# Two-layer streaming encoder on one core: mixer keys set anew, cache rows written from loaded tiles

## The chip, the cores and the metric

One core of a Trainium2 chip runs the whole program; the metric is the device time of one launch in microseconds. The five instruction queues are TensorE (PE), VectorE (DVE), ScalarE (ACT), GpSimd (POOL) and SyncE (SP). In this kernel SP issues every transfer.

## The reference

Two layers act on a prompt of 1024 frames and on a sample batch of 8 streams with 16 frames each. Everything is float32 with 1024 model columns. Cut to what matters:

```python
def trunk_layer(x, ...):
    xn = rms_norm(x, norm_mix)
    q, k, v, u = mixer_inputs(xn, pos, w_in, q_gain, k_gain)
    keys = jnp.concatenate([cache_k, k], axis=1)      # sample; the prompt has no cache
    vals = jnp.concatenate([cache_v, v], axis=1)
    attn = sink_attention(q, keys, vals, sinks, None) # prompt: a window of chunks
    pool, new_pool = pool_mixer(u, pool_prev, w_pool, pool_scale)
    x = x + jnp.concatenate([attn, pool], axis=-1) @ w_out
    f, new_conv = conv_ffn(rms_norm(x, norm_ffn), conv_prev, w_up, conv_w, conv_b, w_down)
    return x + f, keys[:, -WINDOW:], vals[:, -WINDOW:], new_pool, new_conv
```

The last line names what the change touches: for the sample, the new cache of each layer is the newest 112 of the 128 old rows, followed by 16 new ones. The old rows are read for the attention anyway.

## The kernel before, in words

The 1152 rows (1024 prompt, 128 sample) are nine tiles of 128. Each float32 product is made of three TensorE products of rounded high and low parts (`mm3`, L154 to L156), so each weight is split on its way in: a raw block (tag raw, 5 buffers of 256 KB) is cast on ACT (L184) or DVE (L182) to its high part, and DVE takes the low part (L185). The pair (tag W, 6 buffers of 512 KB) is written to DRAM scratch (L188, `wd0k` and the like) and read back from there for the next blocks of tiles (L179).

A layer runs as a **mixer**, then **up**, then **down**. The mixer takes the tiles in three blocks of three: norm (n1 to n3; x tiles loaded at L247, scaled at L258, transposed at L278), key/value/query projections (k0 to k2), pooling input and pooling (u0 to u2, p0 to p2; L448), attention (steps L, per tile: scores L592/L593, masked maximum on DVE L596, exponential on ACT L608, division on DVE L621, transposes L631, value product L644), output projection (o0 to o2) and the second norm (m0 to m2). For the sample tile the scores are at L712, the division at L727, its transposes at L735, the value product at L752; its caches are loaded at L668 and L672. Up and down are products after Strassen's scheme: up forms sums of x halves (s0 and s1; casts L314, subtractions L315, sums L323), multiplies, and adds up the seven products on DVE (L927); down's raw blocks are loaded at L1068 (`wt_load`) and L1078 and split by L1106/L1107, and the hidden rows are split by ACT L1133 and DVE L1134. Layer 0's last ten down units run at the start of layer 1's mixer.

**What sets the order.** The program of a mixer is a list of tokens, each with a key from `PLAN`: `k0=(a, b)` means that step i of stream k0 has the key a + b·i. `arrange` sorts by key as far as prerequisites and buffer limits allow. Then a scheduler sets the order of each engine's queue from that program, and it may hoist an instruction far ahead: the cache copies of both layers stand at 22 to 30 us of the run. PE, DVE and ACT work through their queues in order. SP too: a transfer whose wait is not over holds everything behind it. A transfer also waits for the one eight places ahead of it, since there are eight completion semaphores, used in turn. PSUM has four mm buffers, two s and two tr.

In each `PLAN` entry `e_w` gives how many of every four weight casts go to DVE; `e_k`, `e_u` and their like choose between DVE and ACT for the copies of one step.

Of the kernel before, what the change touches and what calls it, by code (L numbers as in the profile page):

```python
# [44 lines left out]
def arrange(tokens, limits):  # L45
# [17 lines left out]


PLAN = [
    dict(k0=(-17.62, 0.24), u0=(10.61, 1.71), k1=(30.79, 2.26), u1=(78.0, 4.62), o0=(92.76, 2.89), k2=(148.67, 0.53), u2=(167.09, 2.77), o1=(177.0, 4.18), o2=(235.82, 4.28), p0=(40.1, 4.11), p1=(87.53, 9.52), p2=(194.05, 11.9), n1=(-17.77, 3.16), n2=(24.42, 3.62), n3=(92.75, 0.67), m0=(218.99, 3.57), m1=(259.62, 0.1), m2=(181.18, 1.22), d=(4.13, 4.36), L=(26.9, 49.72, 64.52, 85.1, 108.8, 144.29, 159.45, 183.94, 209.44, 245.41), cw=(276.93, 6.24), sc=(242.61, 32.45), s0=(252.65, 2.67), s1=(279.21, 6.7), v=(236.08, 0.18), w=(265.61, 1.32), upw=(297.57, 0.58), e_q=0, e_k=1, e_v=1, e_u=0, e_k2=0, e_qt=0, e_pt0=0, e_pt1=1, e_ps0=1, e_ps1=1, e_ks=0, e_w=1, e_x0=0, e_x1=0, e_x2=1),
    dict(k0=(-52.3, 0.11), u0=(39.12, 0.62), k1=(27.74, 4.1), u1=(77.36, 4.61), o0=(81.16, 2.69), k2=(144.54, 0.53), u2=(154.52, 4.44), o1=(176.58, 5.19), o2=(244.07, 2.25), p0=(50.25, 5.11), p1=(72.82, 0.77), p2=(195.1, 13.29), n1=(-13.38, 2.12), n2=(30.2, 4.39), n3=(93.86, 2.01), m0=(219.6, 1.94), m1=(237.49, 1.8), m2=(278.02, 1.14), d=(-26.81, 5.35), L=(26.9, 49.72, 64.52, 87.91, 107.72, 142.58, 160.43, 180.13, 216.19, 239.71), cw=(266.26, 12.19), sc=(271.63, 4.65), s0=(264.1, 2.05), s1=(266.18, 3.7), v=(283.58, 0.14), w=(284.07, 11.47), upw=(287.29, 0.87), e_q=1, e_k=1, e_v=0, e_u=1, e_k2=0, e_qt=0, e_pt0=0, e_pt1=0, e_ps0=1, e_ps1=1, e_ks=0, e_w=1, e_x0=0, e_x1=1, e_x2=0),
]


# [1 line left out]
def encoder_kernel(ctx: ExitStack, tc: tile.TileContext, consts, x_prompt, x_sample, cache_k, cache_v,  # L72
# [4 lines left out]
    pe, act, dve, pool, sync = nc.tensor, nc.scalar, nc.vector, nc.gpsimd, nc.sync  # L77
# [583 lines left out]
    def sample(l):  # L661
        H = {}
        t = 8
        pr = prep(l, 8)

        def load():
            H["ck"] = T("B", [128, 8, 128])
            sync.dma_start(out=H["ck"], in_=cache_k[l].rearrange("b t g d -> t b (g d)"))  # L668

        def loadv():  # L670
            H["cv"] = T("B", [128, 8, 128])
            sync.dma_start(out=H["cv"], in_=cache_v[l].rearrange("b t g d -> t b (g d)"))  # L672
# [525 lines left out]
    def down_units(l):  # L1198
        us = []
        for u, (j, p) in enumerate(DSEQ):  # L1200
            n = 5 if j in (0, 1, 5, 6) else 4
            late = j == 5 and l < DEPTH - 1
            loads, splits = ((0, 2, 4, 5, 6), (0, 0, 2, 4, 5)) if n == 5 else ((0, 2, 4, 6), (0, 0, 2, 4))

            def f(u=u, j=j, p=p, n=n, late=late, loads=loads, splits=splits):
                if u == 0:
                    down_x(l, 0)
                if u + 2 < len(DSEQ):
                    g_load(l, u + 2)
                if u + 1 < len(DSEQ):  # L1210
                    down_x(l, u + 1)
                    g_split(l, u + 1)
                down_add(l, u, None)
                if j < 6 and not late:
                    for x in range(*(splits + (6,))[p:p + 2]):
                        wd_split(l, j + 1, x)
                    for x in range(*(loads + (6,))[p:p + 2]):
                        wd_load(l, j + 1, x)
                if j == 0:
                    for x in range(p, 6 if p == 4 else p + 1):  # L1220
                        wt_load(l, x)
# [23 lines left out]
    def params1(l):  # L1245
        def f():
            if "own" not in state:
                state["own"] = True
                dve.tensor_reduce(out=own, in_=ident.rearrange("p (b t) -> p b t", t=16), axis=mybir.AxisListType.X, op=ALU.add)
            sync.dma_start(out=gain[:, 0], in_=q_norm[l].partition_broadcast(128))  # L1250
            sync.dma_start(out=gain[:, 1], in_=k_norm[l].partition_broadcast(128))
            sync.dma_start(out=snk[:, 0], in_=attn_sinks[l].partition_broadcast(128))
            for h in range(8):
                sync.dma_start(out=snk[h * 16:(h + 1) * 16, 2, 0:1], in_=attn_sinks[l, h:h + 1].partition_broadcast(16))
            r = T("D", [4, 128])
            sync.dma_start(out=r, in_=pool_scale[l].rearrange("(g p) -> g p", p=128))
            dve.tensor_scalar(out=gain[:, 0], in0=gain[:, 0], scalar1=HD ** -0.5, scalar2=None, op0=ALU.mult)
            dve.tensor_scalar(out=snk[:, 1], in0=snk[:, 0], scalar1=-1.0, scalar2=None, op0=ALU.mult)
            dve.tensor_scalar(out=snk[:, 3, 0:1], in0=snk[:, 2, 0:1], scalar1=-1.0, scalar2=None, op0=ALU.mult)
            tr = P("tr")  # L1260
            pe.transpose(out=tr[:, 0:4], in_=r, identity=ident[0:4, 0:4])
            act.copy(out=pscol, in_=tr[:, 0:4])
        return f
# [71 lines left out]
        x_load(0, [1, 2])()  # L1335
        sync.dma_start(out=cst[:, C_M:C_END], in_=consts[:, C_M:C_END])

    def copies(l):
        def f():
            sync.dma_start(out=nk_s[l, :, 0:112], in_=cache_k[l, :, 16:128])  # L1340
            sync.dma_start(out=nv_s[l, :, 0:112], in_=cache_v[l, :, 16:128])
        return f

    events = []
    pend = []
    for l in range(DEPTH):
        pl = PLAN[l]
        toks = []

        def add(name, key, unit, pre=(), res=None):  # L1350
            toks.append(Token(key, name, unit if isinstance(unit, Unit) else Unit(unit), tuple(pre), res))
# [155 lines left out]
```

## Time and profile before

| | before |
|---|---|
| median of 3 runs | 2243.28 us (2240.95 to 2246.43) |
| the profiled execution | 2242.44 us, span 2240.7 us |
| mean granted clock of TensorE over the span | 0.988 |
| PE busy | 2169.5 us, 97% |
| DVE, ACT, POOL busy | 1712.6 (76%), 943.5 (42%), 326.6 (15%) |
| bytes moved | 389.64 MB, 174 GB/s mean |

Along the span: layer 0's mixer takes 0 to about 420 us, up to 880, down to about 1120; layer 1's mixer (with the end of layer 0's down) to about 1510, up to 1980, down to the end. A row of the timeline gives start, length, engine, line, operation, output <- input, and in brackets how long the engine had been idle and what released it. A granted clock of 1.00 is the full 2.4 GHz, and 0.91 is a mean of stretches at 2.4 and at 1.2 GHz.

### The profile page before, as it was taken

The page shows a single profiled execution, that of the slowest core. Times are in us where ns is not written, and L with a number is a line of the kernel's source. Part 1 is how long each engine was busy: PE and PEld are TensorE (multiplying, and loading weights), DVE is VectorE, ACT ScalarE, POOL GpSimd, SP SyncE. Part 2 cuts the span into 40 slices and gives each one's busy share as a digit, 9 for nine tenths or more (in the row PEclk, how much of TensorE's full clock was granted, in tenths as well). Part 3 has the DMA queues.
Part 4 walks back from the last instruction along what each step waited for, and adds up shares of the span by engine and source line. Part 5 has one row for each costly group of instructions (what it writes and reads, how often), then busy time and mean ns, then how long its engine had stood idle before and what let it go on. Part 6 is the DMA issues. An engine that isn't in the chain of part 4 may idle for free.

```text
span 2240.7 us, 36002 instructions
## 1 busy us (share of the span) xinstructions
PE 2169.5 (97%) x13178; PEld 1945.5 (87%) x13178; DVE 1712.6 (76%) x3234; ACT 943.5 (42%) x1749; POOL 326.6 (15%) x499
## 2 busy tenths in 40 slices
PE   7999999899999999999999999979999999999999
PEld 6867777899999999878888887779999999988887
DVE  4776467989899998867557754689989999987663
ACT  3454345534343434443335543554343434353341
POOL 0000001121213232000000000111212233320000
PEclk9999999899999999999999999999999999999999
DMA  8757565122224346958765665532222343488663
GB/s 313 255 194 269 182 218 173 59 95 79 95 88 151 117 151 220 298 178 268 243 228 184 230 230 207 205 116 84 94 82 93 110 140 128 143 274 267 182 199 113
DMA packets 315940, 389.64 MB, mean 174 GB/s; under 512 B 21906, under 2 KB 219746, under 8 KB 315730
## 3 DMA queue, kind: packets, MB, share of 16 engines
q1 hardware_dynamic: 315762, 387.33, 52.2%
q8 instruction: 104, 1.70, 0.3%
q14 instruction: 74, 0.61, 0.1%
HBM read 279.71 MB, written 109.37 MB: 174 GB/s over the span
## 4 chain that ended last, share of the span: by engine, by line
PE 85%; DMA 6%; DVE 5%; ACT 2%; issue 1%; SPq 0%; POOL 0%; DVEq 0%; ACTq 0%
PE mm L154 15%; PE mm L155 15%; PE mm L156 15%; PE s L156 11%; PE s L154 11%; PE s L155 11%; PE s L644 2%; DMA raw<-in_w_down_dram 1%; DMA raw<-in_w_in_dram 1%; PE tr L631 1%; PE mm L448 1%; DMA W<-wd1o 1%; PE s L592 1%; DMA xd<-u 1%; PE tr L294 1%
## 5 line engine op out<-in xcount | busy, mean ns | idle before, releaser
L154 PE MATMUL mm<-B,W 128*128 128x288 f32 (+1 forms) x1376 | 422.1, 307 | 13.6 <-DVE B L927 7.7
L155 PE MATMUL mm<-B,W 128*128 128x288 f32 (+1 forms) x1376 | 419.2, 305 | 1.9 <-DVE B L315 1.8
L156 PE MATMUL mm<-B,W 128*128 128x288 f32 (+1 forms) x1376 | 417.2, 304 | 0.0
L154 PE MATMUL s<-B,B 128*128 128x512 f32 x704 | 279.6, 397 | 4.1 <-ACT B L1133 2.7
L156 PE MATMUL s<-B,B 128*128 128x512 f32 x704 | 279.2, 397 | 2.8 <-DVE B L1134 2.8
L155 PE MATMUL s<-B,B 128*128 128x512 f32 x704 | 278.6, 396 | 0.0
L154 PEld LDWEIGHTS mm<-B,W 128*128 128x128 f32 x1376 | 262.6, 191 | 17.9 <-DVE B L927 7.9
L155 PEld LDWEIGHTS mm<-B,W 128*128 128x128 f32 x1376 | 262.0, 190 | 3.4 <-DVE B L315 2.4
L156 PEld LDWEIGHTS mm<-B,W 128*128 128x128 f32 x1376 | 261.7, 190 | 1.0 <-DVE W L185 0.4
L975 DVE SCALAR_TENSOR_TENSOR B<-B,cvp,B 128x1168 f32<-128x1168 f32 x176 | 250.6, 1427 | 1.8 <-ACT B L973 1.5
L154 PE MATMUL mm<-W,B 128*128 128x512 f32 (+1 forms) x576 | 220.0, 388 | 12.4 <-ACT W L184 3.1
L155 PE MATMUL mm<-W,B 128*128 128x512 f32 (+1 forms) x576 | 214.8, 374 | 0.2 <-DVE W L185 0.2
L156 PE MATMUL mm<-W,B 128*128 128x512 f32 (+1 forms) x576 | 213.9, 374 | 0.0
L868 ACT CAST W<-Q 128x512 fp32r<-128x512 f32 x132 | 82.0, 621 | 258.1 <-PE mm L156 169.3
L1133 ACT CAST B<-B 128x256 fp32r<-128x256 f32 (+1 forms) x128 | 97.3, 780 | 204.7 <-DMA B<-gd 70.5
L154 PE MATMUL s<-B,W 128*128 128x288 f32 x576 | 171.2, 297 | 1.8 <-ACT B L314 1.2
L155 PE MATMUL s<-B,W 128*128 128x288 f32 x576 | 170.5, 296 | 0.0
L156 PE MATMUL s<-B,W 128*128 128x288 f32 x576 | 170.3, 296 | 0.0
L154 PEld LDWEIGHTS s<-B,B 128*128 128x128 f32 x704 | 133.2, 189 | 36.2 <-ACT B L1133 5.3
L156 PEld LDWEIGHTS s<-B,B 128*128 128x128 f32 x704 | 133.0, 189 | 34.9 <-DVE B L1134 3.6
L155 PEld LDWEIGHTS s<-B,B 128*128 128x128 f32 x704 | 133.1, 189 | 30.7
L869 DVE TENSOR_TENSOR W<-Q,W 128x512 fp32r<-128x512 f32 x132 | 134.6, 1020 | 20.6 <-ACT W L868 20.6
(236 smaller groups left out, 4855.8 us busy)
## 6 DMA issues: line engine op xcount, KB each, us to landing
raw<-in_w_up_dram SPq DMA_DIRECT2D x176, 256.0 KB
raw<-in_w_down_dram SPq DMA_DIRECT2D x154, 256.0 KB
gd<-B SPq DMA_DIRECT2D x44, 576.0 KB
B<-gd SPq DMA_DIRECT2D x32, 576.0 KB
W<-wd0o SPq DMA_DIRECT2D x32, 512.0 KB
W<-wd1o SPq DMA_DIRECT2D x32, 512.0 KB
W<-wd0k SPq DMA_DIRECT2D x24, 512.0 KB
W<-wd1k SPq DMA_DIRECT2D x24, 512.0 KB
```

What stands on the lines that cost most here:

```text
L154: pe.matmul(out=out, lhsT=a[0], rhs=b[0], start=first, stop=False)
L155: pe.matmul(out=out, lhsT=a[0], rhs=b[1], start=False, stop=False)
L156: pe.matmul(out=out, lhsT=a[1], rhs=b[0], start=False, stop=last)
L294: pe.transpose(out=tr[:, k * 128:(k + 1) * 128], in_=xn[:, c:c + 128], identity=ident)
L448: pe.matmul(out=o, lhsT=w.raw, rhs=d, start=True, stop=True)
L592: pe.matmul(out=p[:, i, kr], lhsT=q[:, h], rhs=K[:, g, kr], start=True, stop=False)
L631: pe.transpose(out=tr[:, h * 128:(h + 1) * 128], in_=S[:, h, kk * 128:(kk + 1) * 128], identity=ident)
L644: pe.matmul(out=o, lhsT=V, rhs=H.pop(("p", g, kk)), start=kk == kks[0], stop=kk == 1)
L868: act.copy(out=hi, in_=src)
L869: dve.tensor_tensor(out=lo, in0=src, in1=f32(hi), op=ALU.subtract)
L975: dve.scalar_tensor_tensor(out=c, in0=h[:, j:j + 1168], scalar=cvp[:, j, ct:ct + 1], in1=c, op0=ALU.mult, op1=ALU.add)
L1133: act.copy(out=h, in_=f32(o))
```

## The change

Four edits; line numbers from L669 on rise by two.

1. Every stream of both mixers gets new keys. Among the engine choices, layer 0 changes e_k, e_u, e_k2, e_pt1 and e_w (1 to 0: all its weight casts on ACT, before every fourth on DVE), layer 1 e_q, e_k, e_v and e_u.
2. The 112 old rows of each cache were copied from DRAM to DRAM (L1340, L1341, four transfers of 448 KB). Now each is written from the tile that L668 or L672 has loaded, right behind that load in the program.
3. The tile of pool scales moves from tag D (2 buffers) to tag V.
4. The raw B22 blocks for down's sums (`wt_load`) are begun in units 2 to 4 of the first product, before in units 0 to 4.

```diff
-    dict(k0=(-17.62, 0.24), u0=(10.61, 1.71), ..., n2=(24.42, 3.62), ..., e_w=1, ...),
-    dict(k0=(-52.3, 0.11), u0=(39.12, 0.62), ..., s1=(266.18, 3.7), v=(283.58, 0.14), w=(284.07, 11.47), ...),
+    dict(k0=(12.35, 0.15), u0=(27.6, 1.13), ..., n2=(26.8, 3.63), ..., e_w=0, ...),
+    dict(k0=(-43.86, 0.15), u0=(49.49, 0.1), ..., s1=(276.75, 4.45), v=(278.27, 0.1), w=(272.47, 516.37), ...),
...
             sync.dma_start(out=H["ck"], in_=cache_k[l].rearrange("b t g d -> t b (g d)"))
+            sync.dma_start(out=nk_s[l, :, 0:112].rearrange("b t g d -> t b (g d)"), in_=H["ck"][16:128])
...
             sync.dma_start(out=H["cv"], in_=cache_v[l].rearrange("b t g d -> t b (g d)"))
+            sync.dma_start(out=nv_s[l, :, 0:112].rearrange("b t g d -> t b (g d)"), in_=H["cv"][16:128])
...
                 if j == 0:
-                    for x in range(p, 6 if p == 4 else p + 1):
+                    for x in range(max(2 * p - 4, 0), max(2 * p - 2, 0)):
                         wt_load(l, x)
...
-            r = T("D", [4, 128])
+            r = T("V", [4, 128])
             sync.dma_start(out=r, in_=pool_scale[l].rearrange("(g p) -> g p", p=128))
...
-    def copies(l):
-        def f():
-            sync.dma_start(out=nk_s[l, :, 0:112], in_=cache_k[l, :, 16:128])
-            sync.dma_start(out=nv_s[l, :, 0:112], in_=cache_v[l, :, 16:128])
-        return f
...
-        add("copy", pl["o1"][0], copies(l))
```

How the queues stand now, at three places.

**SP at the start.** After the first eight transfers (x tiles 0 to 2, constants, two raw weight blocks, the norm gain) SP goes on so, before:

```order
L218 DMA raw_248<-in_w_in_dram 128x512
L218 DMA raw_250<-in_w_in_dram 128x512
L218 DMA raw_252<-in_w_in_dram 128x512
L188 DMA wd0k_86<-W_254 128x1024
L218 DMA raw_258<-in_w_in_dram 128x512
L1250 DMA gain<-in_q_norm_dram 128x64
L1251 DMA gain<-in_k_norm_dram 128x64
L188 DMA wd0k_87<-W_260 128x1024
L218 DMA raw_264<-in_w_in_dram 128x512
L1252 DMA snk<-in_attn_sinks_dram 128x8
```

and now:

```order
L1252 DMA gain<-in_q_norm_dram 128x64
L1253 DMA gain<-in_k_norm_dram 128x64
L1254 DMA snk<-in_attn_sinks_dram 128x8
L1256 DMA snk<-in_attn_sinks_dram 16x1 x8
L1258 DMA V_266<-in_pool_scale_dram 4x128
L218 DMA raw_274<-in_w_in_dram 128x512
L218 DMA raw_276<-in_w_in_dram 128x512
L218 DMA raw_278<-in_w_in_dram 128x512
L188 DMA wd0k_86<-W_280 128x1024
L218 DMA raw_284<-in_w_in_dram 128x512
L188 DMA wd0k_87<-W_286 128x1024
L247 DMA B_248<-in_x_prompt_dram 128x1024
```

Twelve small loads of parameters (gain, snk, pool scales) have come ahead of the third raw block. The three loads of x tiles 3 to 5 (B_248 is the first) stand in front of the seventh raw block, before behind the sixteenth, and the four cache copies that stood between the weights are gone.

**PE at the scores of prompt tiles of layer 0, about 140 us.** The last score (L593) of the later of two tiles, the projections' matmuls that follow (mm), and the transposes (L631) that need the earlier tile's divided scores B_1342, before:

```order
L593 MATMUL s_1386<-B_1021,Q_1304 128x256
L155 MATMUL mm_1673<-W_1840,B_1036 128x512
L156 MATMUL mm_1673<-W_1840,B_1036 128x512
L155 MATMUL mm_1677<-W_1840,B_1279 128x512
L156 MATMUL mm_1677<-W_1840,B_1279 128x512
L631 MATMUL tr_1422<-cst,B_1342 128x128
L631 MATMUL tr_1429<-cst,B_1342 128x128
```

and now, from the same score on:

```order
L593 MATMUL s_1386<-B_922,Q_1304 128x256
L155 MATMUL mm_1673<-W_1754,B_1014 128x512
L156 MATMUL mm_1673<-W_1754,B_1014 128x512
L155 MATMUL mm_1677<-W_1754,B_1279 128x512
L156 MATMUL mm_1677<-W_1754,B_1279 128x512
L154 MATMUL mm_1673<-W_1812,B_1014 128x512
L154 MATMUL mm_1677<-W_1812,B_1279 128x512
L155 MATMUL mm_1673<-W_1812,B_1014 128x512
L156 MATMUL mm_1673<-W_1812,B_1014 128x512
L155 MATMUL mm_1677<-W_1812,B_1279 128x512
L156 MATMUL mm_1677<-W_1812,B_1279 128x512
L154 MATMUL mm_1673<-W_1840,B_1014 128x512
```

Five more matmuls like the last one follow before the same transposes. So 16 of them stand between that score and the transposes, before 4. Counted from the earlier tile's own last score (s_1351), 36 stand there, before 18.

**DVE where layer 1's mixer turns into up, about 1490 us.** The last rows of the second norm (L258), the x sums (L315, L323) and the additions of up's products (L927, now L929), before:

```order
L258 SCALAR_TENSOR_TENSOR B_15665<-B_15325,st_15666,B_15029 128x1024
L258 SCALAR_TENSOR_TENSOR B_15671<-B_15327,st_15672,B_15029 128x1024
L315 TENSOR_TENSOR B_15698<-B_15443,B_15697 128x1152
L315 TENSOR_TENSOR B_15702<-B_15451,B_15701 128x1152
L315 TENSOR_TENSOR B_15771<-B_15695,B_15770 128x1152
L323 TENSOR_TENSOR B_15695<-B_15687,B_15695 128x1152
L323 TENSOR_TENSOR B_15687<-B_15443,B_15687 128x1152
L315 TENSOR_TENSOR B_15776<-B_15695,B_15775 128x1152
L927 TENSOR_TENSOR B_15795<-mm_15782,PT_15756 128x288
L323 TENSOR_TENSOR B_15443<-B_15695,B_15443 128x1152
L927 TENSOR_TENSOR PT_15756<-s_15800,PT_15756 128x288
L323 TENSOR_TENSOR B_15451<-B_15451,B_15443 128x1152
```

and now:

```order
L258 SCALAR_TENSOR_TENSOR B_15740<-B_15325,st_15741,B_15050 128x1024
L258 SCALAR_TENSOR_TENSOR B_15746<-B_15327,st_15747,B_15050 128x1024
L929 TENSOR_TENSOR PT_15680<-s_15707,PT_15680 128x288
L929 TENSOR_TENSOR PT_15738<-mm_15725,PT_15680 128x288
L929 TENSOR_TENSOR PT_15680<-mm_15779,PT_15680 128x288
L929 TENSOR_TENSOR B_15793<-mm_15779,PT_15738 128x288
L929 TENSOR_TENSOR B_15698<-mm_15862,PT_15680 128x288
L315 TENSOR_TENSOR B_15812<-B_15443,B_15811 128x1152
L315 TENSOR_TENSOR B_15816<-B_15451,B_15815 128x1152
L315 TENSOR_TENSOR B_15845<-B_15178,B_15844 128x1152
L871 TENSOR_TENSOR W_15967<-raw_15944,W_15967 128x512
L929 TENSOR_TENSOR B_15698<-mm_15914,PT_15680 128x288
```

Before, six x sums (L315, L323) stood between the last L258 and the first addition, and more between the additions. Now five additions follow the last L258 at once, one more stands already ahead of it, and those sums come later.

Two more moves need no rows. In layer 0 the transfer of layer 1's pool scales (L1256), which stood between the first two B22 loads (L1068), now stands some 30 places later. The B22 loads keep their places in SP's queue in both layers, since the scheduler hoists them to where a W buffer comes free. The cache writes stand three places behind their load or less, with reads of W (L179) behind them.

## Rows read from the trace of the kernel before

**Rows 1.** Page: busy us by engine, and the closing chain's shares.

```profile
PE 2169.5 (97%) x13178; PEld 1945.5 (87%) x13178; DVE 1712.6 (76%) x3234; ACT 943.5 (42%) x1749; POOL 326.6 (15%) x499
...
PE 85%; DMA 6%; DVE 5%; ACT 2%; issue 1%; SPq 0%; POOL 0%; DVEq 0%; ACTq 0%
```

**Rows 2.** Stages: length; PE, PEld, DVE, ACT, POOL busy (count); PEclk; DMA share.

```profile
120.00:160.00 40.00, 35.39 (x161) 24.96 (x161) 24.25 (x84) 19.20 (x53) 2.89 (x2) 0.91 0.44 156
240.00:280.00 40.00, 36.71 (x197) 28.79 (x196) 14.80 (x40) 12.01 (x38) 1.96 (x1) 0.97 0.54 174
280.00:320.00 40.00, 38.04 (x195) 30.18 (x194) 25.45 (x80) 16.78 (x53) 2.32 (x1) 0.94 0.70 238
440.00:480.00 40.00, 40.00 (x303) 39.97 (x302) 36.37 (x62) 14.34 (x22) 7.40 (x16) 1.00 0.28 91
880.00:920.00 40.00, 37.70 (x174) 30.88 (x173) 30.90 (x44) 21.59 (x34) 7.39 (x7) 0.96 1.02 325
1480.00:1520.00 40.00, 28.68 (x191) 27.03 (x190) 37.38 (x52) 20.68 (x31) 8.00 (x10) 0.87 0.18 59
```

**Rows 3.** Timeline of PE, 42 to 60 us: start, length, instruction, [idle <-releaser].

```profile
43.65 0.51 PE L154 MATMUL mm<-W,B 128*128 128x256 f32 x2 [2.34 <-ACT W L184]
...
59.52 1.54 PE L278 MATMUL tr<-cst,B 128*128 128x128 f32 x6 [3.02 <-DVE B L258]
```

**Rows 4.** Timeline of the SP queue, 14 to 45 us.

```profile
14.41 5.97 SPq L1254 DMA_DIRECT2D snk<-in_attn_sinks_dram  x7
...
22.60 0.81 SPq L1340 DMA_DIRECT2D out_dram<-in_cache_k_dram  x1
...
44.21 2.30 SPq L247 DMA_DIRECT2D B<-in_x_prompt_dram  x3
```

**Rows 5.** Waits of the SP queue: us in total, times, longest.

```profile
SPq L1256 <- POOL B L961: 4.2, 1, 4.2
...
SPq L218 <- DMA out_dram<-in_cache_v_dram: 3.5, 2, 1.9
...
SPq L188 <- DMA out_dram<-in_cache_k_dram: 1.9, 1, 1.9
```

**Rows 6.** Timeline of PE, 135 to 147 us.

```profile
135.46 0.28 PE L593 MATMUL s<-B,Q 128*128 128x256 f32 x1
...
140.46 0.40 PE L156 MATMUL mm<-W,B 128*128 128x512 f32 x1
143.53 1.35 PE L631 MATMUL tr<-cst,B 128*128 128x128 f32 x8 [2.68 <-DVE B L621]
146.35 0.69 PE L556 MATMUL tr<-cst,ks 128*128 128x128 f32 x2 [1.47 <-ACT PT L151]
```

**Rows 7.** Timeline of PE, 271 to 278 us.

```profile
271.20 0.71 PE L712 MATMUL s<-B,Q 64*64 64x144 f32 x8
...
276.64 0.66 PE L735 MATMUL tr<-cst,B 128*128 128x128 f32 x4 [1.78 <-DVE B L727]
...
277.98 0.46 PE L400 MATMUL tr<-cst,B 120*128 120x120 f32 x1 [0.57 <-ACT B L736]
```

**Rows 8.** Timeline of PE, 312 to 325 us.

```profile
312.73 0.50 PE L154 MATMUL mm<-W,B 128*128 128x512 f32 x1 [1.68 <-DMA W<-wd0o]
...
324.72 0.39 PE L592 MATMUL s<-B,Q 128*128 128x256 f32 x1 [1.19 <-DVE B L649]
```

**Rows 9.** Timeline of PE, 886 to 889 us.

```profile
886.72 0.50 PE L154 MATMUL s<-B,B 128*128 128x512 f32 x1 [0.92 <-ACT B L1133]
...
888.83 0.79 PE L156 MATMUL s<-B,B 128*128 128x512 f32 x1 [1.38 <-DVE B L1134]
```

**Rows 10.** Timeline of DVE, 1498 to 1500 us.

```profile
1498.69 1.35 DVE L315 TENSOR_TENSOR B<-B,B 128x1152 fp32r<-128x1152 f32 x1
1499.95 0.45 DVE L927 TENSOR_TENSOR B<-mm,PT 128x288 f32<-128x288 f32 x1
```

**Rows 11.** Timeline of PE, 1500 to 1501 us.

```profile
1500.46 0.61 PE L154 MATMUL mm<-B,W 128*128 128x288 f32 x1 [7.67 <-DVE B L927]
```

More of the change, by code (lines that the diff above doesn't have):

```diff
@@ L65 @@
 PLAN = [
-    dict(k0=(-17.62, 0.24), u0=(10.61, 1.71), k1=(30.79, 2.26), u1=(78.0, 4.62), o0=(92.76, 2.89), k2=(148.67, 0.53), u2=(167.09, 2.77), o1=(177.0, 4.18), o2=(235.82, 4.28), p0=(40.1, 4.11), p1=(87.53, 9.52), p2=(194.05, 11.9), n1=(-17.77, 3.16), n2=(24.42, 3.62), n3=(92.75, 0.67), m0=(218.99, 3.57), m1=(259.62, 0.1), m2=(181.18, 1.22), d=(4.13, 4.36), L=(26.9, 49.72, 64.52, 85.1, 108.8, 144.29, 159.45, 183.94, 209.44, 245.41), cw=(276.93, 6.24), sc=(242.61, 32.45), s0=(252.65, 2.67), s1=(279.21, 6.7), v=(236.08, 0.18), w=(265.61, 1.32), upw=(297.57, 0.58), e_q=0, e_k=1, e_v=1, e_u=0, e_k2=0, e_qt=0, e_pt0=0, e_pt1=1, e_ps0=1, e_ps1=1, e_ks=0, e_w=1, e_x0=0, e_x1=0, e_x2=1),
@@ L67 @@
-    dict(k0=(-52.3, 0.11), u0=(39.12, 0.62), k1=(27.74, 4.1), u1=(77.36, 4.61), o0=(81.16, 2.69), k2=(144.54, 0.53), u2=(154.52, 4.44), o1=(176.58, 5.19), o2=(244.07, 2.25), p0=(50.25, 5.11), p1=(72.82, 0.77), p2=(195.1, 13.29), n1=(-13.38, 2.12), n2=(30.2, 4.39), n3=(93.86, 2.01), m0=(219.6, 1.94), m1=(237.49, 1.8), m2=(278.02, 1.14), d=(-26.81, 5.35), L=(26.9, 49.72, 64.52, 87.91, 107.72, 142.58, 160.43, 180.13, 216.19, 239.71), cw=(266.26, 12.19), sc=(271.63, 4.65), s0=(264.1, 2.05), s1=(266.18, 3.7), v=(283.58, 0.14), w=(284.07, 11.47), upw=(287.29, 0.87), e_q=1, e_k=1, e_v=0, e_u=1, e_k2=0, e_qt=0, e_pt0=0, e_pt1=0, e_ps0=1, e_ps1=1, e_ks=0, e_w=1, e_x0=0, e_x1=1, e_x2=0),
+    dict(k0=(12.35, 0.15), u0=(27.6, 1.13), k1=(35.46, 2.26), u1=(78.0, 4.62), o0=(92.76, 2.89), k2=(160.39, 1.54), u2=(167.47, 3.15), o1=(177.0, 4.09), o2=(235.74, 4.2), p0=(40.1, 3.5), p1=(86.68, 12.45), p2=(194.05, 11.9), n1=(-86.25, 2.26), n2=(26.8, 3.63), n3=(92.6, 1.1), m0=(218.99, 3.57), m1=(260.89, 0.13), m2=(181.58, 0.95), d=(-13.48, 3.86), L=(26.9, 49.72, 64.52, 85.45, 108.8, 144.29, 158.38, 183.7, 209.44, 245.41), cw=(259.88, 23.53), sc=(227.68, 60.94), s0=(257.44, 3.18), s1=(268.93, 2.61), v=(209.05, 0.65), w=(316.25, 1.16), upw=(342.36, 0.16), e_q=0, e_k=0, e_v=1, e_u=1, e_k2=1, e_qt=0, e_pt0=0, e_pt1=0, e_ps0=1, e_ps1=1, e_ks=0, e_w=0, e_x0=1, e_x1=0, e_x2=0),
@@ new lines @@
+    dict(k0=(-43.86, 0.15), u0=(49.49, 0.1), k1=(26.26, 4.1), u1=(76.32, 4.61), o0=(81.16, 2.69), k2=(139.16, 1.11), u2=(150.18, 5.15), o1=(175.45, 5.19), o2=(244.07, 2.25), p0=(49.92, 3.56), p1=(56.81, 4.29), p2=(193.02, 12.48), n1=(-18.93, 0.85), n2=(30.53, 4.46), n3=(92.15, 1.8), m0=(222.0, 1.72), m1=(234.28, 0.33), m2=(278.02, 1.14), d=(-24.93, 3.08), L=(26.9, 49.72, 64.52, 87.91, 106.15, 148.52, 158.51, 180.13, 216.19, 239.71), cw=(264.41, 12.12), sc=(273.99, 6.32), s0=(264.1, 2.08), s1=(276.75, 4.45), v=(278.27, 0.1), w=(272.47, 516.37), upw=(298.18, 0.41), e_q=0, e_k=0, e_v=1, e_u=0, e_k2=0, e_qt=0, e_pt0=0, e_pt1=0, e_ps0=1, e_ps1=1, e_ks=0, e_w=1, e_x0=0, e_x1=1, e_x2=0),
```

## The prediction

> **What bounds the kernel now.** I read the page first. PE is busy for 2169.5 us of the 2240.7 and carries 85% of the closing chain; DVE has 1712.6 us and ACT 943.5 [rows 1]. So the kernel is bound by TensorE, and the change neither adds nor removes a matmul worth counting. What it can win is PE's lost time, and that lies in a few places. The table by stage shows them: in the up phase PE is busy for 40.00 of 40 us at a clock of 1.00, so nothing is to be had there, while five other stretches lose something [rows 2]. The loss has two parts, the idle time and the time at the lower clock. With the mean clock as a measure, a stretch loses about (40 − PE busy) + 40 × (1 − PEclk): at 120 to 160 us 4.6 + 3.6 = 8.2 us, at 240 to 280 us 3.3 + 1.2 = 4.5, at 280 to 320 us 2.0 + 2.4 = 4.4, at 880 to 920 us 2.3 + 1.6 = 3.9, and at 1480 to 1520 us 11.3 + 5.2 = 16.5 [rows 2]. An idle of 2 to 3 us thus costs about twice its length, as the clock falls behind it. Then I read the timeline of PE for what ended each idle stretch, and the queues for what stood in front of that.
>
> **The change, part by part.** Only places where the order differs can change.
>
> *Scores at 140 us (keys of layer 0).* The earlier tile's last score starts at 135.46 and its transposes at 143.53, so scores, maximum, exponential and division take 8.1 us; the matmuls between them cover only 5 us, and PE idles 2.68 us for the division (L621), then 1.47 us for ACT's copy [rows 6]. The matmuls there repeat every 0.23 us (0.40 us each, overlapped). Before, 18 of them and 8 scores stand between: 18 × 0.23 + 0.9 = 5.1 us. Now it is 36: 36 × 0.23 + 0.9 = 9.2 us, more than 8.1. The later tile's scores now come later, too, and on DVE the division of the earlier one stands behind them, so some 0.4 us may stay idle. I take −5.5 us out of the 8.2 (bounds −7 and −1: the latter if the chain is stretched as much as the cover).
>
> *Sample scores at 271 us.* The last sample scores start at 271.20, their transposes at 276.64 after 1.78 us of idle; 0.57 and more follow, since the next transposes wait for ACT [rows 7]. The order now has 18 matmuls in that gap with 0.6 us of other work, 4.8 us, against 9 (2.1 us) before, and the chain from the end of the scores took 276.64 − 271.91 = 4.7 us. The two stretches around it lose 8.9 us [rows 2]; I leave 3.4 to other stalls in them and take −5.5 us (−7, −1).
>
> *Tile scores at 312 to 325 us.* The DMA wait of 1.68 us for an output weight has the same place in both orders and stays. Some 16 matmuls come between two groups of scores where PE now waits 1.19 us for DVE [rows 8]: −1 us (−3, +1).
>
> *Start.* Two idle stretches should go. At 59.52 PE waits 3.02 us for the normed x tile 3 [rows 3], whose load is issued at 44.21 behind the weights [rows 4]; it now stands ten weight blocks earlier in the queue. At 43.65 it waits 2.34 us for a weight block [rows 3]. The four cache copies are gone from this queue; weight traffic there waited 3.5 + 1.9 us for them [rows 5]. Against that, twelve small parameter loads stand ahead of the third raw block. Seven such loads held the queue for 5.97 us, 0.85 us each, at 14.41 [rows 4]; twelve at that rate are 10.2 us. PE wants the third block only behind the products of the first two, so I count that it comes 2 us late and PE loses as much (0 to 7, the latter nearer to the row). Sum: −3.0 and −2.3 for the idle, about −2 for the clock behind it, +2 at the beginning, and +2 since the x loads now compete with the weights: −3 us (−8, +4).
>
> The Trainium skill (DMA: Bandwidth & Descriptors, Rules for kernel authors and Anatomy of one DMA) speaks against this part: it says that a transfer under 64 KB is mostly overhead, and gives each about 2.0 us fixed. By that, as an estimate, twelve small loads over eight completion semaphores hold the weights for 12 × 2.0 / 8 = 3 us, 1 us more than I take, and the sum would be 1 us higher; the row of the trace, whose seven waited for large transfers ahead of them, makes it dearer still.
>
> *Cache rows from loaded tiles.* The writes wait on the SP queue for their load, with reads of weights behind them. A wait for a transfer of that size was 1.9 us at most [rows 5], so the four cost up to 7.6 us of SP's time. The weight read behind is wanted some 80 matmuls, about 16 us, after its buffer is free, which covers it: 0 (0, +4: half of that time uncovered). In bytes, 4 × 448 KB are read less.
>
> *Pool scales in tag V.* Before, SP waited 4.2 us at this transfer for POOL's copy of the tile in D [rows 5], with down's first weights behind it. From there on the DMA engines are full (1.02 of their time at 880 to 920 us [rows 2]), and PE waits 0.92 and 1.38 us for down's first blocks [rows 9]. The wait goes, and the queue of loads starts up to 4.2 us sooner: −2 us (−4, 0). For layer 1 there is no such transfer.
>
> *Raw B22 blocks begun later.* The loads have the same places on SP: 0. If the program position did count, a load begun one unit later would have to hurt at the switch from up to down, where 3.9 us are lost already; I bound it by +2.
>
> *From mixer to up, layer 1.* PE idles 7.67 us until DVE's first addition (L927) [rows 11], which starts at 1499.95 right behind a subtraction of 1.35 us that PE does not need yet [rows 10]. Six such sums, 8 us, stood ahead. Now the additions go first, so PE's next products start about 9 us earlier. But DVE is busy for 37.38 of 40 us here [rows 2]; the sums for the second half are only deferred, and PE will wait for these 5 to 6 us later: −3.5 us (−8, 0).
>
> *Casts on ACT in layer 0, other choices.* ACT is 42% busy: 0 (−1, +2). New stalls from an order that I cannot follow by hand in every place: the old one has a dozen of 0.5 to 1.8 us; I add +3.5 (0, +8).
>
> Sum: −5.5 − 5.5 − 1 − 3 + 0 − 2 + 0 − 3.5 + 0 + 3.5 = −17.0 us. The profiled execution took 2242.44 us, 0.84 us below the median of the runs shown, 2243.28; so the forecast is **2225.4 us**, 0.8% faster.
>
> **The rivals.** *Starved start (same).* The twelve small loads cost the full 7 us, the early x loads push the weights back by another 4, and the idle at 43.65 grows instead of going. For it: the queue is held for 0.85 us by each small load [rows 4]. Against: the copies free the queue of as much. Price: the start at +8 instead of −3, so 2236.4 us, just within 0.3% (6.7 us).
>
> *Stalls are only shifted (same).* The scores' chains stretch with the new order, since DVE takes its work in another order too, and the products at the layer-1 boundary wait as long for the x sums as before for the additions. For it: DVE's 37.38 us at that boundary. Against: at 140 and 271 us DVE is only 14.8 to 24.3 us busy in 40 [rows 2]. Price: −1 − 1 − 1 − 3 − 2 + 0 + 3.5 = −4.5, 2238 us.
>
> *Weights late in layer 0's mixer (slower).* The matmuls that now fill the gaps are products with streamed weights, so they come up earlier than before, while the six W buffers and the queue, with cache writes in it, have not become faster. Then PE waits for weights instead of for DVE. One such wait was 1.68 us [rows 8], and about as much goes to the clock: 3.4 us. Ten of the some forty reads of that mixer late by this much are +34 us; against −17 that gives 2259 us. It decides from seven late reads (+24, slower by 6.8 us). Against it: the DMA share there is 0.44 to 0.70, so the engines have room [rows 2].
>
> *The change does not do what it says.* For the B22 blocks I hold this for likely, and it is in the sum as 0.
>
> **How the numbers follow.** Forecast 0.72; starved start 0.08; only shifted 0.12; weights late 0.08. 0.3%, 6.7 us, is about what a measurement of this kernel tells from no change. The forecast's own range is from 2212 (start and both score places at their good ends, no new stall: −30) to 2235 (half of the gains); with the two neutral cases it reaches to 2240, and 0.1 lies above it and 0.06 below 2211. Faster by over 0.3% is most of the forecast and a little of the rivals, 0.75; within 0.3% 0.16; slower 0.09.
>
> **What would show it.** After the change, PE at about 140 and 271 us without idle of over 0.5 us; none at tile 3's transposes near 59 us; no wait of SP at the pool scales; the 7.67 us gone at the layer-1 boundary and an idle of some 5 us before a later product in its place; the boundary of layer 0 near 400 us as before. The prediction is wrong if PE's idle in layer 0's mixer is released by reads of W, or if the first 60 us end later than now.

## The result, and the profile after

The changed kernel takes 2228.72 us (median of 4 runs, 2225.27 to 2231.4), the kernel before 2242.11 us beside it (2239.06 to 2246.43): a ratio of 0.9933, 95% interval 0.9916 to 0.995. That is 13.4 us faster; 17.0 were forecast, and the time lies inside the range of 2211 to 2240. The profiled execution has a span of 2229.6 us, 11.1 less than before. One execution of a later run, that with layer 1's old keys, took 4297.6 us, about twice as long as its five others, and is left out of its median.

The page of the changed kernel, busy us by engine and the closing chain's shares, against [rows 1]:

```profile
PE 2163.0 (97%) x13178; PEld 1939.9 (87%) x13178; DVE 1698.6 (76%) x3198; ACT 958.7 (43%) x1785; POOL 325.1 (15%) x499
...
PE 79%; DMA 11%; DVE 5%; ACT 2%; issue 2%; SPq 1%; DVEq 0%; ACTq 0%
```

PE has the same 13178 matmuls. The shares of the chain moved from PE (85% to 79%) to transfers (6% to 11%), though no transfer was added; no run shows why.

The table by stage, with the same columns as [rows 2] (the last number of a row is GB/s moved); the last two stretches begin 12 and 10 us earlier than there, since the program runs that much ahead:

```profile
120.00:160.00 40.00, 37.27 (x186) 28.41 (x185) 30.16 (x110) 23.13 (x66) 4.47 (x3) 1.00 0.64 226
240.00:280.00 40.00, 39.23 (x210) 31.08 (x209) 18.73 (x58) 14.43 (x45) 3.32 (x2) 1.00 0.68 222
280.00:320.00 40.00, 36.85 (x190) 27.85 (x191) 29.20 (x98) 21.43 (x65) 1.95 (x1) 1.00 0.52 185
440.00:480.00 40.00, 40.00 (x305) 40.00 (x304) 36.05 (x61) 16.87 (x23) 7.77 (x18) 1.00 0.29 95
868.00:908.00 40.00, 37.54 (x166) 30.51 (x166) 31.78 (x44) 20.95 (x33) 7.27 (x7) 0.91 1.02 325
1470.00:1510.00 40.00, 31.56 (x200) 29.57 (x199) 35.67 (x47) 22.62 (x35) 6.22 (x9) 0.87 0.14 40
```

With the prediction's measure, idle time plus 40 × (1 − PEclk), 120 to 160 us now lose 2.7 us (before 8.2), 240 to 280 us 0.8 (4.5), 280 to 320 us 3.2 (4.4), the start of down 2.5 + 3.6 = 6.1 (3.9), and the boundary of layer 1 8.4 + 5.2 = 13.6 (16.5).

How far the changed kernel is ahead, and where, shows at places that both kernels pass in the same way. The first is PE's wait of 1.73 us at layer 0's switch from mixer to up, before and then changed:

```profile
393.45 0.43 PE L154 MATMUL mm<-B,W 128*128 128x288 f32 x1 [1.73 <-ACT B L314]
```

```profile
383.23 0.40 PE L154 MATMUL mm<-B,W 128*128 128x288 f32 x1 [1.73 <-ACT B L314]
```

There it is 10.2 us ahead. At down's first product, 886.72 [rows 9] against 874.51 below, it is 12.2 us ahead, and at the end 11.1. So layer 0's mixer makes most of the gain. Some 2 us come in up, where PE is busy all the time in both (305 matmuls in 40 us against 303); what makes them is not shown. What lies behind loses 1.1 in this execution. A second execution of the changed kernel (below) is 9.8 us ahead at the first place and 14.3 at the end, so the part behind the mixer varies by some 3 us.

PE's timeline of the changed kernel at the two score places, against [rows 6] and [rows 7]:

```profile
138.51 1.23 PE L631 MATMUL tr<-cst,B 128*128 128x128 f32 x8
140.99 0.66 PE L556 MATMUL tr<-cst,ks 128*128 128x128 f32 x4 [1.25 <-ACT PT L151]
...
279.89 0.66 PE L737 MATMUL tr<-cst,B 128*128 128x128 f32 x4 [0.56 <-ACT B L738]
```

The transposes at 138.51 find their operands ready; the idle of 2.68 us is gone, one of 1.25 before the next transposes is left, where the prediction wanted none above 0.5. At the sample scores 0.56 is left of 1.78 and 0.57.

The start, as two stretches of 60 and 40 us, of the kernel before and then of the changed kernel (columns as above):

```profile
0.00:60.00 60.00, 42.50 (x219) 36.79 (x220) 27.07 (x59) 20.00 (x38) 4.81 (x10) 0.96 0.87 317
60.00:100.00 40.00, 39.28 (x213) 32.94 (x213) 30.07 (x105) 22.62 (x60) 3.32 (x3) 0.97 0.71 259
```

```profile
0.00:60.00 60.00, 45.52 (x251) 40.12 (x252) 31.28 (x68) 25.75 (x53) 4.85 (x10) 1.00 0.86 311
60.00:100.00 40.00, 37.57 (x193) 30.41 (x192) 28.04 (x96) 19.62 (x52) 3.28 (x3) 0.96 0.65 233
```

PE gets 251 matmuls into the first 60 us, before 219. The two idle stretches of [rows 3] are gone. But the first products are late; SP's queue and PE's timeline of the changed kernel:

```profile
9.40 5.57 SPq L1256 DMA_DIRECT2D snk<-in_attn_sinks_dram  x8
...
15.42 1.30 SPq L218 DMA_DIRECT2D raw<-in_w_in_dram  x3
```

```profile
14.14 0.80 PE L154 MATMUL mm<-W,B 128*128 128x512 f32 x1 [1.74 <-ACT B L281]
...
17.25 0.69 PE L278 MATMUL tr<-cst,B 128*128 128x128 f32 x2 [1.89 <-DVE B L282]
...
72.52 0.87 PE L278 MATMUL tr<-cst,B 128*128 128x128 f32 x6 [1.37 <-DVE B L258]
```

The third weight block is issued at 15.42, behind the small loads, and PE idles 1.89 us at 17.25, and 1.37 us at 72.52. What releases PE at 17.25 is a DVE copy (L282). DVE's timeline shows what that copy stood behind, a scaling of the sinks that waits for their load:

```profile
16.57 0.15 DVE L1261 TENSOR_SCALAR snk<-snk 128x1 f32<-128x1 f32 x1 [1.73 <-DMA snk<-in_attn_sinks_dram]
16.64 1.01 DVE L282 TENSOR_TENSOR B<-tr,B 128x384 fp32r<-128x384 f32 x2
```

At the pool scales, SP's waits in the changed kernel between 845 and 860 us, against [rows 5], and PE's at down's first products, against [rows 9]:

```profile
SPq L1070 <- PE mm L156: 7.4, 2, 4.6
```

```profile
874.51 0.50 PE L154 MATMUL s<-B,B 128*128 128x512 f32 x1 [1.07 <-ACT B L1135]
...
876.63 0.79 PE L156 MATMUL s<-B,B 128*128 128x512 f32 x1 [1.39 <-DVE B L1136]
```

SP no longer waits for POOL, but the load of weights behind it (L1070, before L1068) waits 4.6 us for PE to free a W buffer. PE's two idle stretches are there as before.

The boundary of layer 1 (where its mixer turns into up), PE of the changed kernel, against [rows 11]:

```profile
1473.38 0.61 PE L154 MATMUL mm<-B,W 128*128 128x288 f32 x1 [2.24 <-ACT B L314]
...
1492.36 0.40 PE L154 MATMUL mm<-B,W 128*128 128x288 f32 x1 [3.92 <-ACT B L314]
1494.31 0.61 PE L155 MATMUL mm<-B,W 128*128 128x288 f32 x1 [1.56 <-DVE B L315]
```

The 7.67 us are gone; in their place stand 3.92 us for a cast on ACT and 1.56 us for a subtraction on DVE, 5.5 us together.

### The profile page after: what moved, and what is told of

Read it like the earlier page. It is cut to its first block, busy times and chain, and to the rows that moved or that the text cites. A ratio compares the mean times of both kernels' runs of the same rounds, so it can differ in the third digit from the quotient of the medians.

```text
span 2229.6 us, 36029 instructions
## 1 busy us (share of the span) xinstructions
PE 2163.0 (97%) x13178; PEld 1939.9 (87%) x13178; DVE 1698.6 (76%) x3198; ACT 958.7 (43%) x1785; POOL 325.1 (15%) x499
## 2 busy tenths in 40 slices
DMA packets 319524, 389.64 MB, mean 175 GB/s; under 512 B 21938, under 2 KB 223362, under 8 KB 319346
## 4 chain that ended last, share of the span: by engine, by line
PE 79%; DMA 11%; DVE 5%; ACT 2%; issue 2%; SPq 1%; DVEq 0%; ACTq 0%
PE mm L154 16%; PE mm L155 15%; PE mm L156 15%; PE s L156 9%; PE s L154 9%; PE s L155 9%; DMA raw<-in_w_down_dram 2%; PE s L644 2%; DMA u<-xd 1%; DMA B<-gd 1%; DMA out_dram<-u 1%; DMA B<-sd1S 1%; DMA W<-wd0o 1%; PE tr L631 1%; PE mm L448 1%
## 5 line engine op out<-in xcount | busy, mean ns | idle before, releaser
L154 PEld LDWEIGHTS mm<-B,W 128*128 128x128 f32 x1376 | 261.1, 190 | 15.9 <-ACT B L314 12.2
L154 PE MATMUL mm<-W,B 128*128 128x512 f32 (+1 forms) x576 | 217.0, 384 | 11.4 <-DMA W<-wd0o 3.5
```

The lines of the kernel that those rows point to most:

```text
L154: pe.matmul(out=out, lhsT=a[0], rhs=b[0], start=first, stop=False)
```

## The experiments

Two theories. A: the gain lies in the order of layer 0's mixer, by its keys. B: it lies in the cache copies that are gone, or in layer 1. All ratios are to runs of the kernel before on the same chip; the interval is the 95% one.

**Layer 0's keys alone.**

```diff
 PLAN = [
-    dict(k0=(-17.62, 0.24), ...  # layer 0, before
+    dict(k0=(12.35, 0.15), ...   # layer 0, changed
```

> The kernel before with layer 0's PLAN entry of the change alone (cache copies, tag D, early B22 loads and layer 1's keys as before). Theory A, the gain lies in the order of layer 0's mixer: 9 to 12 us faster, near 2231 us, and the trace some 10 us ahead when layer 0's up begins; no idle of over 0.5 us at the transposes near 140 us. Rival B, the gain lies in the cache traffic and in layer 1: at most 4 us faster.

Measured: 2230.21 us, ratio 0.9956 (0.9941 to 0.997). As theory A has it, 9.6 us of gain without any of the other edits; PE's wait at the switch to up ends at 385.30, 8.2 us ahead. The transposes of the scores (L631) wait no more, but the 1.25 us before the next ones are there as in the changed kernel. The start shows that none of it comes from there:

```profile
0.00:60.00 60.00, 43.35 (x220) 37.25 (x221) 27.20 (x56) 24.42 (x50) 4.48 (x10) 0.97 0.86 311
60.00:100.00 40.00, 37.12 (x193) 30.73 (x192) 30.67 (x102) 19.20 (x52) 3.56 (x3) 0.96 0.63 233
```

220 matmuls in 60 us are the 219 of before, and (idle and clock) the first 100 us lose 22.9 us against 21.8.

**Layer 1's keys alone.**

```diff
-    dict(k0=(-52.3, 0.11), ...   # layer 1, before
+    dict(k0=(-43.86, 0.15), ...  # layer 1, changed
```

> The kernel before with layer 1's PLAN entry of the change alone. Theory A: 1 to 2 us faster, near 2240.5 us; at the switch from layer 1's mixer to up the idle of 7.67 us is replaced by two or three that together have 5 to 6 us and are released by ACT L314 and DVE L315. Rival, the wait is gone and not shifted: 4 us or more faster, less than 3 us of idle there.

Measured: 2240.65 us against 2239.84, ratio 1.0001 (0.9991 to 1.001): no gain, where theory A had 1 to 2 us. PE's timeline at the boundary has the shifted waits, 3.93 + 1.34 = 5.3 us, as theory A had it:

```profile
1477.75 0.40 PE L154 MATMUL mm<-B,W 128*128 128x288 f32 x1 [2.23 <-ACT B L314]
...
1495.27 0.61 PE L154 MATMUL mm<-B,W 128*128 128x288 f32 x1 [3.93 <-ACT B L314]
1497.22 0.61 PE L155 MATMUL mm<-B,W 128*128 128x288 f32 x1 [1.34 <-DVE B L315]
```

**The cache edit alone.**

```diff
+            sync.dma_start(out=nk_s[l, :, 0:112]..., in_=H["ck"][16:128])
+            sync.dma_start(out=nv_s[l, :, 0:112]..., in_=H["cv"][16:128])
-        add("copy", pl["o1"][0], copies(l))
```

> The kernel before with the cache rows written from the loaded tiles alone, keys as before. Theory A: the copies leave the start, so the idle of 2.34 us at 43.65 goes with the clock behind it, 2 to 4 us faster, near 2239 us; the idle of 3.02 us near 59.5 us stays, and no wait for W grows behind the cache writes. Rival B, the copies cost more than that since the start is bound by transfers: 5 us or more faster. Rival C, the writes hold the queue for weights: 2 us or more slower in layer 0's mixer.

Measured: 2228.44 us, ratio 0.9949 (0.9934 to 0.9964), 11.4 us faster. Theory A's 2 to 4 us fell: the copies cost more, and rival B has it right here. The start:

```profile
0.00:60.00 60.00, 47.79 (x261) 42.39 (x262) 35.08 (x81) 23.25 (x45) 5.36 (x10) 1.00 0.91 327
60.00:100.00 40.00, 38.83 (x232) 32.69 (x231) 25.81 (x94) 21.04 (x56) 4.08 (x3) 1.00 0.66 245
```

261 matmuls in 60 us, the clock at 1.00, and 13.4 us lost in 100 us instead of 21.8. That is 8.4 us of the 11.4; where the rest is won is not shown. The idle near 59.5 us went too, though the x tiles are loaded at their old place behind the weights. At the scores near 135 us PE still idles 2.69 us, since the keys are the old ones:

```profile
135.21 1.81 PE L631 MATMUL tr<-cst,B 128*128 128x128 f32 x8 [2.69 <-DVE B L621]
```

**Pool scales and B22 blocks alone.**

```diff
-            r = T("D", [4, 128])
+            r = T("V", [4, 128])
-                    for x in range(p, 6 if p == 4 else p + 1):
+                    for x in range(max(2 * p - 4, 0), max(2 * p - 2, 0)):
```

> The kernel before with the pool scales in tag V and the later B22 blocks alone. Theory A: no difference beyond 2 us; SP no longer waits at the pool scales, but for PE at the next B22 load (L1068) by about as much, so down's first transfers start at the same time and PE's idle of 0.92 and 1.38 us near 887 us stays. Rival, as predicted: 2 to 4 us faster, those two idle stretches gone.

Measured: 2240.74 us against 2239.84, ratio 1.0006 (0.9996 to 1.0015): nothing, as theory A had it. The two loads behind the pool scales are issued at 866.14 us, before at 866.64, and a load ahead of them at 845.67 and 846.18, so the queue of loads starts no sooner. SP's wait there, and PE's at down's first products:

```profile
SPq L1068 <- PE mm L156: 7.4, 2, 4.7
```

```profile
885.86 0.50 PE L154 MATMUL s<-B,B 128*128 128x512 f32 x1 [0.56 <-ACT B L1133]
...
887.95 0.80 PE L156 MATMUL s<-B,B 128*128 128x512 f32 x1 [1.36 <-DVE B L1134]
```

**Bytes or places?** What of the copies costs the start is told apart by copies that move little from the same places.

```diff
-            sync.dma_start(out=nk_s[l, :, 0:112], in_=cache_k[l, :, 16:128])
+            sync.dma_start(out=nk_s[l, :, 0:1], in_=cache_k[l, :, 16:17])
```

(and the same for v)

> The kernel before with its four cache copies cut to one row of each stream (8 x 128 elements instead of 8 x 14336), at the same places of the SP queue; 111 of the 112 old rows are left out of the new caches. Theory D, what the copies cost at the start is their bytes on the full transfer engines: both idle stretches of PE (2.34 us near 43.65, 3.02 us near 59.5) go, 7 to 11 us faster than before, like the run without copies. Rival, their places in the queue and the waits on the completion semaphores cost it: at most 3 us faster, SP still waits some 5 us in the start for the copies.

Measured: 2232.76 us against 2240.98, ratio 0.9959 (0.9944 to 0.9974), 8.2 us faster. The start of this run, then 44 to 60 us of it and of the kernel before:

```profile
0.00:60.00 60.00, 47.18 (x260) 42.10 (x261) 34.41 (x80) 23.14 (x45) 4.82 (x10) 1.00 0.88 318
60.00:100.00 40.00, 38.84 (x228) 32.28 (x227) 25.83 (x93) 20.66 (x55) 4.08 (x3) 1.00 0.69 256
```

```profile
44.00:60.00 16.00, 16.00 (x98) 15.96 (x97) 13.38 (x38) 6.04 (x13) 2.48 (x2) 1.00 1.04 388
```

```profile
44.00:60.00 16.00, 12.76 (x68) 12.28 (x67) 9.49 (x24) 4.18 (x8) 2.48 (x2) 0.87 1.02 388
```

260 matmuls in 60 us, as without copies. From 44 to 60 us the transfer engines are full in both (1.04 and 1.02, 388 GB/s), but before PE idled 3.2 us of these 16 at a clock of 0.87: the copies' 1.8 MB had stood among the weights. In the first 60 us both kernels move the same 19.1 MB, so this one gets 1.8 MB more of its own loads and writes through. No wait of SP for a copy is left; the waits of [rows 5] were the bytes' doing, not the places'. Whether the bytes cost PE by filling the transfer engines, or by holding SP until they had landed, is not told apart: both went together. What the four places cost by themselves is within the noise: the next run, on the same chip, is 3.1 us faster, but the intervals overlap.

**No writes at all** (against the kernel of the cache edit alone; the old rows are left out of the new caches):

```diff
-            sync.dma_start(out=nk_s[l, :, 0:112]..., in_=H["ck"][16:128])
-            sync.dma_start(out=nv_s[l, :, 0:112]..., in_=H["cv"][16:128])
```

> The kernel before without the copies and without the writes from loaded tiles; the old rows are left out of the new caches. Theory D: the writes are hidden, so it takes as long as the kernel with writes alone changed, 2228.5 us within 2 us. Rival C, the writes hold weights up behind them: 3 us or more faster than that kernel, near 2225 us.

Measured: 2229.62 us, ratio 0.9954 (0.9935 to 0.9973), no better than the 0.9949 of the run with the writes. The writes cost nothing that shows within the interval of some 4 us either way; rival C falls.

**The parameters later.**

```diff
-            add("par", 10, params1(0))
+            add("par", 13.5, params1(0))
```

> The changed kernel with the token of layer 0's parameters at key 13.5 instead of 10, so that the small loads come behind the first weight blocks. Theory E, the small loads ahead of the third weight block cost the changed kernel its 1.89 us of idle at 17.25 us and the late weights: 2 to 4 us faster than the changed kernel, near 2225.5 us, first 30 us with 2 to 3 us less loss. Rival: the same time within 1.5 us, since the x loads that still stand early hold the weights up as well.

Measured: 2227.99 us, ratio 0.9942 (0.9924 to 0.9961); in a second set of more rounds

> The run with the parameters' token at 13.5 once more, with more rounds. Theory E: 2 to 4 us faster than the changed kernel beside it, since its first 100 us lost 5 us less. Rival: no difference beyond 1.5 us, what is won at the start is lost again before the end.

2228.75 us, ratio 0.9937 (0.992 to 0.9954), beside the changed kernel once more:

> The changed kernel once more, as the measure for the next three on the same chip: 2228.5 us within 1.5 us, 11 to 14 us faster than before.

2227.33 us, ratio 0.9938 (0.9915 to 0.9962), by the medians 15.4 us faster than the kernel before. So moving the parameters makes no difference, though the start is better, 14.5 us lost in 100 us instead of 18.5:

```profile
0.00:60.00 60.00, 48.22 (x271) 43.09 (x272) 35.06 (x78) 27.52 (x55) 4.49 (x10) 1.00 0.92 337
60.00:100.00 40.00, 37.28 (x214) 30.56 (x212) 27.66 (x101) 20.60 (x59) 5.09 (x4) 1.00 0.59 217
```

271 matmuls in 60 us against 251. By the medians nothing of it is left at the end. With this one key the scheduler set other orders in far places as well: in both profiled executions PE idles 2.39 us before a value product of layer 1, where the changed kernel has under 0.5, a place where some of it can have gone. PE of the second execution:

```profile
1431.98 2.08 PE L644 MATMUL s<-PT,V 128*128 128x512 f32 x2 [2.39 <-ACT PT L151]
...
2056.29 0.77 PE L154 MATMUL s<-B,B 128*128 128x512 f32 x1 [3.04 <-ACT B L1135]
```

The second row shows a place that varies with the execution: 3.04 us here at layer 1's down, released through ACT by a load, and 0.53 us in the first execution of the same kernel.

**The old start keys, the new rest.**

```diff
-k0=(12.35, 0.15), u0=(27.6, 1.13), n1=(-86.25, 2.26), n2=(26.8, 3.63)
+k0=(-17.62, 0.24), u0=(10.61, 1.71), n1=(-17.77, 3.16), n2=(24.42, 3.62)
```

> The changed kernel with the four streams of the start (n1, n2, k0, u0 of layer 0) at their old keys. Theory E, without the copies the old start order is the better one (the run with the cache edit alone lost 6 us at 10 to 100 us, the changed kernel 12), and the new order of the later mixer keeps its gain: 4 to 7 us faster than the changed kernel, near 2223 us. Rival: the later order hangs on the new start keys; no faster than 2227 us.

Measured: 2229.26 us, ratio 0.9942 (0.9923 to 0.9961); the rival holds. The start is as good as without copies (13.8 us lost in 100 us), but at the scores PE idles again:

```profile
134.51 1.76 PE L631 MATMUL tr<-cst,B 128*128 128x128 f32 x7 [2.69 <-DVE B L621]
```

**n2 at its old key** (and the parameters later):

```diff
-n2=(26.8, 3.63)
+n2=(24.42, 3.62)
```

> As the run before, and the second norm of layer 0 (n2) at its old key 24.42. Theory F, PE's idle of 1.53 us at tile 3's transposes near 69 us comes from n2's later key on DVE: it goes, and the time is 2 to 3 us less than the run before. Rival: the idle moves to the scores near 140 us, same time within 1.5 us.

Measured: 2225.44 us, ratio 0.9921 (0.9903 to 0.9938). The idle near 69 us is gone, and the one at the scores is back, so theory and rival each have one half right. The start, the stretch at the scores, and PE there:

```profile
0.00:60.00 60.00, 47.82 (x271) 42.62 (x272) 35.58 (x77) 28.18 (x57) 5.34 (x11) 1.00 0.93 337
60.00:100.00 40.00, 39.13 (x234) 33.05 (x233) 27.81 (x108) 20.47 (x60) 4.48 (x3) 1.00 0.63 227
120.00:160.00 40.00, 34.93 (x179) 26.94 (x178) 31.10 (x109) 25.30 (x70) 4.47 (x3) 1.00 0.57 199
```

```profile
133.72 1.23 PE L631 MATMUL tr<-cst,B 128*128 128x128 f32 x8 [2.68 <-DVE B L621]
```

The median is 3.3 us below that of the run before it and 1.9 us below the changed kernel's on the same chip, but the intervals overlap; whether it beats them stays open. It is at least no slower, with the wait back that the change was to remove.

**Layer 1's old keys** (and the parameters later):

```diff
+    dict(k0=(-52.3, 0.11), ...   # layer 1, before
```

> As the run with the parameters' token at 13.5, and layer 1's PLAN entry as before. Theory A, layer 1's keys only shift the wait at the switch to up: same time within 1.5 us, the idle of 7.67 us back. Rival, they are worth the predicted 3.5 us: 3 to 4 us slower than with them.

Measured: 2225.9 us, ratio 0.9921 (0.9903 to 0.9939): not slower than the 2228.75 with the new keys, with the old wait back:

```profile
1464.37 0.40 PE L154 MATMUL mm<-B,W 128*128 128x288 f32 x1 [2.57 <-ACT B L314]
...
1474.33 0.66 PE L294 MATMUL tr<-cst,B 128*128 128x128 f32 x4 [0.88 <-ACT B L300]
1482.66 0.61 PE L154 MATMUL mm<-B,W 128*128 128x288 f32 x1 [7.68 <-DVE B L929]
```

## Why the prediction was right, and where it was off

The terms below are in the prediction's measure, and each is read from one execution.

*Scores at 140 and 271 us.* Forecast −5.5 and −5.5. The stretch at 120 us lost 5.5 us less, those from 240 to 320 us 4.9 less. Covering the chain with matmuls worked as counted: from the earlier tile's last score to the transposes PE is busy throughout. But that −5.5 came out so exactly is in part luck. Only 1.9 us of it are idle time; 3.6 are the clock of 0.91 before, and that part differs between executions. The waits at 140 us stand as before in the run with layer 1's keys alone, and its row shows a clock of 0.96, so 1.6 us:

```profile
120.00:160.00 40.00, 34.62 (x161) 24.31 (x160) 25.35 (x89) 20.07 (x56) 3.92 (x2) 0.96 0.46 161
```

In the run with n2 at its old key PE idles the same 2.68 us at the transposes and the clock stays at 1.00. So it is not a rule that an idle of 2 to 3 us costs twice its length; with that wait in place the clock cost 0 to 3.6 us in this stretch. The 4.9 us likewise hold 3.6 of clock; the other part is 1.3 of idle.

*Start.* Forecast −3, by 7.3 off and 4 on. The first 100 us lose 14.5 + 2.4 + 1.6 = 18.5 us, before 21.8: −3.3. The sum came out, its parts did so only in part. The working gave the vanished idle at 59.52 to the x loads that stand earlier, and it went with the copies alone, by their bytes; that run loses 8.4 us less. The new start order then gives back 5.1 (18.5 against 13.4). The small loads make 4.0 of it, where +2 was forecast: the run that moves them loses 14.5. With n2 at its old key as well the loss is 13.1, so the rest is the second norm's place on DVE. The early x loads, +2 in the forecast, cost nothing that shows: in that last run they are issued at 20.40 us, before at 44.21. The cost of the small loads came by another way also, through DVE, which waited for the sinks with PE's operand behind it.

The Trainium skill (DMA: Bandwidth & Descriptors, Anatomy of one DMA) gave an estimate of 3 us for the small loads; that section is about transfers issued from GpSimd, and here SP issues. The trace has them dearer: eight of them hold SP for 5.57 us, and the third weight block is issued at 15.42 us, before at 4.72, close to the 10.2 us that the prediction worked out for the queue.

*Cache writes.* Forecast 0; the run without them agrees within its interval.

*Pool scales.* Forecast −2, measured 0. The step that failed is that the queue of loads would start 4.2 us sooner; it starts no sooner. The wait had a second one right behind it, hidden by it: the next load of weights needs a W buffer that PE frees at the same time (4.6 us). The trace of before could not show it as a wait, since SP reached that load late; what freed the W buffer had to be asked.

*B22 blocks.* Forecast 0, together with the pool scales 0.

*Boundary of layer 1.* Forecast −3.5 with 5 to 6 us of idle in a later place. The idle came as said, 5.5 us; the stretch lost 2.9 us less. As a whole layer 1's keys are worth nothing that can be measured, so the rest of that layer loses what the boundary wins; where, the executions do not tell alike.

*The other places, and the measure.* Forecast +3.5 in all. The four terms measured make −5.5 − 4.9 − 3.3 − 2.9 = −16.6, where the spans differ by 11.1. The gap is not time lost elsewhere. The same measure over the whole span gives 71.2 us of idle and 26.9 for the clock of 0.988 before, 66.6 and 15.6 for 0.993 after: −15.9. So in that measure the other places together come to +0.7, within the rounding of the clock (one of them, the start of down in layer 0, to +2.2), and the measure itself books 4.8 us too much. The pages show where: of the 11.1 us, 4.6 are idle time and only 6.5 are shorter busy time, while the measure counts 11.3 for the clock. It counts idle time at the lower clock twice, as idle and as slow. By the clock records of the two traces PE was idle for 10.3 of the 55.0 us at the lower clock before, and for 1.7 of 30.7 after; half of that difference is 4.3 us. In the second execution of the changed kernel the measure gives −16.0 and the span is 14.3 us shorter.

Against the trace's −11.1 the sum of −17.0 is thus 5.9 us too much: 4.8 for the measure, 2 for the pool scales, 0.6 each for the sample scores and the boundary, less 0.3 for the start and 1.8 for the other places and the tile scores, where +2.5 was put. Some of the nearness is errors that cancel: the small loads are 2 us dearer and the x loads 2 us cheaper than put, and the reserve for other places was hardly needed while the pool scales gave nothing. The medians differ by 2.3 us more than the two profiled executions do. Two smaller points of the working: its lower end of −30 is −28.5 by its own terms (−17 − 5 − 1.5 − 1.5 − 3.5), and up, where it saw nothing to be had, gave some 2 us.

*The rivals.* The start was not starved: it won 3.3 us. Stalls that are only shifted describe layer 1's boundary and the pool scales, but not the scores. Weights late in layer 0's mixer: up to 385 us PE waits for reads of the output weight (`wd0o`) five times, 3.5 us in all, before three times, 2.6 us; the rival needed seven late reads of 1.68 us, each with its clock. By the letter of the prediction's sign of being wrong some of PE's idle there is released by reads of W, but it was so before. At the tile scores, −1 was forecast; the output weight's wait of 1.68 us [rows 8] has become two in the changed kernel's PE timeline:

```profile
301.95 0.50 PE L154 MATMUL mm<-W,B 128*128 128x512 f32 x1 [0.92 <-DMA W<-wd0o]
...
331.91 0.50 PE L154 MATMUL mm<-W,B 128*128 128x512 f32 x1 [1.50 <-DMA W<-wd0o]
```

Why the edits do not add up is shown in part: 9.6 us for layer 0's keys alone, 11.4 for the cache edit alone, 13.4 for all. With the old order the cache edit wins 8.4 us at the start; with the new one the start wins 3.3, and the new keys' gain is made behind it. The prediction has no such overlap in it, nor that the cache edit alone is worth 11.4 us.

## What to carry to other kernels

A wait on an in-order queue may hide another behind it: before you book its removal, ask what each of the next instructions needs and when that comes free. Transfers whose result no engine needs still cost where the transfer engines are full: move their bytes to a place with room, or feed them from a tile that is loaded anyway. A mean clock beside idle time is a measure of where a kernel loses, not a sum of microseconds: check it against the difference of the spans, and look at a second execution before you price the clock. With a scheduler, an edit of one key moves instructions a thousand microseconds away, so compare whole orders, and take a stretch's gain for the kernel's only when the total agrees.

## What was not expected

Copying 1.8 MB that no engine needs, out of 389.64 MB, cost about 8 us of 2240 (6 to 13 by the interval). Their bytes alone take 4.7 us at the 388 GB/s of that stretch; PE's idle came with a clock of 0.87 in its wake. And the same kernel differs between executions at one place by 2.5 us (0.53 against 3.04 us of idle at layer 1's first down products), about as much as several of the terms argued over here.
